# Latent convolution in 32x32 tiles, a layer norm by channels, and sums over blocks by additions

## The chip, the core and the metric

The kernel runs on one core of a Trainium2 chip. A core has engines that work side by side, each with an instruction stream of its own: TensorE (PE, matrix products on a 128x128 array, with a queue for loading the stationary operand, PEld), VectorE (DVE), ScalarE (ACT), GpSimd (POOL) and SyncE (SP), from whose queue nearly all of this kernel's DMA transfers are issued. Engines wait for each other by semaphores. Data lie on chip in SBUF (128 partitions) and in eight PSUM banks (128 partitions x 512 columns of fp32, where matmuls write), off chip in HBM.

The metric is the time of one execution in microseconds on the device, median of the runs. Less is better.

## What is computed

One layer of a hybrid backbone: an SSD branch (bidirectional Mamba-2 scan) and a Conformer branch share one input projection and one output projection. 256 context tokens and 2048 latent tokens go through it, model width D = 1024, so 18 tiles of 128 tokens. Cut to what the change bears on:

```python
u = (rms_norm(x, g_pre) * (1 + scale) + shift) @ w_in
z, xbc, dt_raw, ga, gb, gsil = split(u)            # 1024 channels each but xbc, dt_raw
y_ssd, h_fin = ssd_branch(z, xbc, dt_raw, ...)     # ends in silu(z) * y, rms_norm over channels

def conformer_branch(ga, gb, conv_w, conv_b, ln_g, ln_b):
    h = ga * sigmoid(gb)
    h = depthwise_conv(h, conv_w, conv_b)          # 31 taps, each channel by itself
    h = layer_norm(h, ln_g, ln_b)                  # over the 1024 channels of a token
    return silu(h)

y_conf = conformer_branch(...) * silu(gsil)
out = concat([y_ssd, y_conf]) @ w_out              # 2048 x 1024
return x + gate * rms_norm(out, g_post), h_fin
```

The 31 taps run along the rows of the grid. The latent grid has 32 rows of 64 columns; so for one channel the convolution is a 32x32 band matrix (Toeplitz: the entry depends on the distance of two rows) times a block of 32 rows by 64 columns. The context grid is 256 rows of one column.

## The kernel before

**Projections.** Tokens come in two halves, each a sequence of blocks of up to 512 tokens. A unit takes the 128 weight columns of one group of channels and goes through the blocks: `mm_cm` (L373) issues, for each of the eight pieces of 128 input channels, three matmuls (L378, L379, L380), since weights and activations are split in a high and a low part of type FP32R. The result is channel-major (channels on partitions). `gab_unit` (L528) projects gate and value of 128 channels j of the Conformer branch, multiplies them and stores the product to the DRAM tensor GL[j]; `silu_unit` does z and gsil, stored to ZS and GS. The weights are fetched on SP's queue by `load_w` (L340), up to three units ahead.

**Beside the projections.** The generators of the scan (`pass_a`, L648) and of the convolutions are woven in between projection steps with `merge` and `interleave` (L836 to L866): after so many steps of projection one step of the side work is issued. For the second half (L926 to L942) these are the scan of tiles 9 to 17 and, from the 49th step on, a chain of `lat_conv(0)`, `ctx_conv(4)`, `lat_conv(1)`, `lat_conv(2)` and so on: all eight groups of latent channels and the last four of the context. In the profile this is the stage from about 935 to 1345 us.

**Context convolution,** `ctx_conv` (L580): 31 fused multiply-adds on DVE, channel-major; two transposes on PE (L595); ACT multiplies by 0.5 (L597); a store to CVC, which is token-major (a token's 1024 channels in a row).

**Latent convolution,** `lat_conv(j)` (L603), 128 channels. kd receives the Toeplitz matrices, by reading the padded taps with overlap (L611); x receives the products from GL[j], the 32 rows of one of four channels on each group of 32 partitions (L616). `expand` (L618) has ACT copy the 32x32 matrices of four channels at a time onto the diagonal of a 128x128 tile in kbuf, whose other entries are zero from the start (16 copies per 128 channels, L622). A matmul (L634) then has x of four channels as the stationary operand (128 partitions by 64 grid columns) and a block-diagonal tile as the moving one (128 columns: four channels by 32 rows). Its result takes 64 columns of the array, so two of them, for the two halves h, write to the two halves of a PSUM bank. There are four groups of eight such matmuls per 128 channels. DVE adds the bias and turns the order of the columns (L639). Two stores put vt to CVL (L644), token-major.

**Output phase.** After the projections comes a loop over the token tiles (L1141 to L1168), latent tiles from the last to the first, then the two of the context. In a turn, PE does 96 matmuls of the output projection for tile i (`out_part`, L1073; 16 pieces of 128 channels, three products, two halves of 512 columns) while other engines prepare the next tiles. The text of the loop sets where the work for the next tile stands between them:

- `ssd_pre` (L968) for the tile after the next: inter-chunk term, y times z, Square on ACT (L989), a sum over eight blocks of channels as one reduction on DVE (L991);
- `ssd_norm` (L1001) and `ssd_scale` (L1010): sum over partitions as a matmul with ones into a column (L1004), the power -0.5 on GpSimd (`rstd_of`, L135), its spread over the partitions by a matmul with the identity (L1012), the multiplication (L1013), the split in high and low parts (`ssd_hl`, L1016);
- `conf_pre` (L1037): load of the tile, token-major (n, tag cn, one buffer), mean and variance by `bn_stats` and `bn_aggr` on DVE (L1042, L1044), L135 on GpSimd, and the normalisation with the two columns of each token as scalars (L1047);
- `conf_act` (L1050): eight transposes back to channel-major (L1058), eight activations with Silu, whose scale and bias are the layer norm's weights by channel (L1061), the product with gsil (L1063); v has one buffer;
- `conf_hl` (L1066): split of v, copy on ACT and L1070 on DVE; `finish` (L1081): the output norm and the store.

Before the loop, the first tile's preparation stands between the last projection units (L1119 to L1132).

**What sets the order.** Each engine runs its own instructions in order. The order is not simply that of the text: the kernel is built in a context with `schedule_with_timeline_sim=True`, in which a list scheduler places instructions by their order in the text and by a simulated time at which their inputs are ready. Buffers come free when their last reader is done; a tile of a pool with `bufs=1` can be loaded again only then. PSUM has three banks with the tag "mm" for projections and five with the tag "ss" for everything else.

## Time and profile before

| | |
|---|---|
| runs | 1882.09, 1887.08 and 1880.9 us; median 1882.09 us |
| profiled execution | 1882.2 us, of which the span from first to last instruction is 1880.5 us |
| mean granted TensorE clock | 0.986 |
| busy | PE 1825.6 us (97%), PEld 1504.6, DVE 1188.2 (63%), ACT 839.5 (45%), POOL 269.0 (14%) |
| DMA | 375.29 MB, 200 GB/s in the mean |

How to read it: an engine's busy time is the sum over its instructions, register and branch instructions left out. The span is the profiled execution's, so a sum of costs taken from the trace is to be set against 1882.2 us. L622 is line 622 of the kernel before; a tile is called by its name in the program without its number (kbuf, cx, cn). A row of a group has: line, engine, operation, output and inputs, shapes, count | busy us, mean ns of one | idle time of the engine just before, and what ended it. A row of the timeline has: start and duration in us, engine, line, operation, output and inputs, shapes, count. The duration of a matmul is its latency; matmuls are pipelined and overlap. An fp32 matmul is recorded as two passes, so its counts are twice those of the code; the matmuls of type FP32R and the transposes are one pass each.

### The profile page before, as it was taken

What the parts mean: (1) busy time and instruction counts of PE and PEld (TensorE: products, weight loads), DVE (VectorE), ACT (ScalarE), POOL (GpSimd) and SP (SyncE); (2) the same over time, 40 slices, a digit from 0 to 9 for tenths busy, and PEclk for the clock granted to TensorE, in tenths of its full rate; (3) what the DMA queues carried; (4) which work ended last, traced back from release to release, by engine and by line L of the source; (5) the groups of instructions that cost most, each with busy time, mean ns of one, the idle gap of its engine ahead of it and who ended that gap; (6) DMA issues with size and microseconds to landing.
All of it is one profiled execution on the core that took longest, in us unless ns stands there. A gap on an engine that the chain in (4) does not pass through costs nothing.

```text
span 1880.5 us, 26833 instructions
## 1 busy us (share of the span) xinstructions
PE 1825.6 (97%) x9739; PEld 1504.6 (80%) x9739; DVE 1188.2 (63%) x1699; ACT 839.5 (45%) x1786; POOL 269.0 (14%) x351
## 2 busy tenths in 40 slices
PE   7899999999999999999999899999999999999998
PEld 4788887787887888888877677777887888888887
DVE  2477887776545553577585768655427676766662
ACT  3646424443455441644355666675414232232321
POOL 0002001111111100100001011110013333333220
PEclk9899999999999999999999999999999999999999
DMA  8556575564677754545587897978887655555532
GB/s 302 212 200 198 211 239 179 176 222 155 211 269 225 225 200 169 165 154 188 179 195 215 210 242 194 278 185 234 239 268 239 191 174 173 165 172 173 175 102 78
DMA packets 290400, 375.29 MB, mean 200 GB/s; under 512 B 85206, under 2 KB 187478, under 8 KB 290268
## 3 DMA queue, kind: packets, MB, share of 16 engines
q1 hardware_dynamic: 290268, 373.58, 64.2%
q8 instruction: 77, 1.26, 0.3%
q14 instruction: 55, 0.45, 0.1%
HBM read 243.92 MB, written 129.59 MB: 199 GB/s over the span
## 4 chain that ended last, share of the span: by engine, by line
PE 62%; DMA 5%; ACT 3%; issue 3%; DVE 2%; SPq 2%; POOL 0%; POOLq 0%; DVEq 0%; ACTq 0%
PE op L1078 20%; PE sp L378 6%; PE sp L379 6%; PE sp L380 6%; DMA lb<-lt 3%; PE xp L379 2%; PE xp L378 2%; PE xp L380 2%; PE py L720 2%; PE ga L378 2%; PE ga L380 1%; PE po L727 1%; PE ga L379 1%; PE qo L985 1%; PE gb L378 1%
## 5 line engine op out<-in xcount | busy, mean ns | idle before, releaser
L684 ACT ACTIVATE lb<-lb,WB 128x128 f32<-128x128 f32 x576 | 184.1, 391 | 150.9 <-POOL lb L676 149.0
L378 PE MATMUL sp<-hh,wh 128*128 128x512 f32 (+1 forms) x640 | 239.7, 375 | 2.6 <-DVE sth L550 2.6
L379 PE MATMUL sp<-hl,wh 128*128 128x512 f32 (+1 forms) x640 | 237.0, 370 | 0.0
L380 PE MATMUL sp<-hh,wl 128*128 128x512 f32 (+1 forms) x640 | 236.7, 370 | 0.2 <-DMA wl<-wld 0.2
L676 POOL TENSOR_SCALAR_AFFINE_SELECT lb<-lb 128x512 f32<-128x512 f32 x144 | 108.7, 760 | 749.7 <-ACT el L673 416.1
L378 PE MATMUL xp<-hh,wh 128*128 128x512 f32 (+1 forms) x480 | 179.1, 375 | 6.1 <-ACT wh L353 4.0
L379 PE MATMUL xp<-hl,wh 128*128 128x512 f32 (+1 forms) x480 | 179.1, 373 | 0.2 <-DVE hl L299 0.2
L380 PE MATMUL xp<-hh,wl 128*128 128x512 f32 (+1 forms) x480 | 179.2, 374 | 0.0
L475 DVE SCALAR_TENSOR_TENSOR cva<-raw,cwh,cva 128x1280 f32<-128x1280 f32 (+1 forms) x96 | 142.7, 1495 | 15.5 <-ACT cva L469 13.6
L378 PEld LDWEIGHTS sp<-hh,wh 128*128 128x128 f32 x640 | 121.0, 189 | 24.3 <-DVE sth L550 3.1
L380 PEld LDWEIGHTS sp<-hh,wl 128*128 128x128 f32 x640 | 121.0, 189 | 21.6 <-DMA wl<-wld 0.7
L379 PEld LDWEIGHTS sp<-hl,wh 128*128 128x128 f32 x640 | 121.2, 189 | 20.1 <-issue 0.5
L378 PE MATMUL gb<-hh,wh 128*128 128x512 f32 (+1 forms) x320 | 121.9, 381 | 3.4 <-DVE gth L539 3.4
L378 PE MATMUL ga<-hh,wh 128*128 128x512 f32 (+1 forms) x320 | 120.4, 376 | 2.6 <-ACT gth L536 2.6
L379 PE MATMUL gb<-hl,wh 128*128 128x512 f32 (+1 forms) x320 | 119.3, 373 | 0.0
L380 PE MATMUL gb<-hh,wl 128*128 128x512 f32 (+1 forms) x320 | 119.1, 372 | 0.0
L380 PE MATMUL ga<-hh,wl 128*128 128x512 f32 (+1 forms) x320 | 118.1, 369 | 0.0
L379 PE MATMUL ga<-hl,wh 128*128 128x512 f32 (+1 forms) x320 | 117.9, 369 | 0.0
L590 DVE SCALAR_TENSOR_TENSOR cg<-cg,cv 128x256 f32<-128x256 f32 x240 | 113.3, 497 | 2.5
L550 DVE SCALAR_TENSOR_TENSOR sth<-sth,sp 128x512 f32<-128x512 f32 (+1 forms) x80 | 50.4, 630 | 98.4 <-ACT sth L549 98.4
L378 PEld LDWEIGHTS xp<-hh,wh 128*128 128x128 f32 x480 | 92.0, 192 | 23.0 <-ACT wh L353 4.8
L688 DVE TENSOR_TENSOR lb<-lb,lb 128x512 f32<-128x512 f32 x72 | 51.6, 717 | 85.6 <-ACT lb L684 55.8
(219 smaller groups left out, 3860.8 us busy)
## 6 DMA issues: line engine op xcount, KB each, us to landing
lb<-lt SPq DMA_DIRECT2D x144, 256.0 KB, 4.2
wr<-in_w_in SPq DMA_DIRECT2D x88, 256.0 KB, 4.9
whd<-wh SPq DMA_DIRECT2D x44, 512.0 KB, 3.4
wld<-wl SPq DMA_DIRECT2D x44, 512.0 KB, 4.7
wh<-whd SPq DMA_DIRECT2D x44, 512.0 KB, 5.2
wl<-wld SPq DMA_DIRECT2D x44, 512.0 KB, 5.6
xT<-xb SPq DMA_DIRECT2D x18, 512.0 KB, 5.4
yp<-yg SPq DMA_DIRECT2D x36, 256.0 KB, 4.5
```

Source lines behind the costliest of these rows:

```text
L378: T.matmul(ps[:, :BN], wh[:, k, :], hh[:, k, :], start=(k == 0), stop=False)
L379: T.matmul(ps[:, :BN], wh[:, k, :], hl[:, k, :], start=False, stop=False)
L380: T.matmul(ps[:, :BN], wl[:, k, :], hh[:, k, :], start=False, stop=(k == KT - 1))
L475: V.scalar_tensor_tensor(a[:, :n], raw[:, t:t + n], cwh[:, ct * 5 + t:ct * 5 + t + 1], a[:, :n], MUL, ADD)
L550: V.scalar_tensor_tensor(th, th, 1.0, ps[:, :BN], ADD, MUL)
L590: V.scalar_tensor_tensor(acc, g[:, t:t + 256], cv[:, w0 + t:w0 + t + 1], acc, MUL, ADD)
L676: G.affine_select(E[g, hq, d], E[g, hq, d], pattern=[[0, 4], [sg, P]], compare_op=ALU.is_ge, fill=NEG, base=0, channel_multiplier=-sg)
L684: S.activation(lb[:, h, :], lb[:, h, :], AF.Exp, bias=WB[:, i, c + h:c + h + 1])
L688: V.tensor_tensor(a, a, E[g, hq, 1], ADD)
L720: T.matmul(py[g][j * HD:(j + 1) * HD, q * P:(q + 1) * P], xt[g][:, h * HD:(h + 1) * HD], E[g, hq, 0][:, t, :], start=True, stop=True)
L727: T.matmul(po[g][:, q * P:(q + 1) * P], Sf[g][:, q * P:(q + 1) * P], bc[:, 2 + g, :], start=True, stop=True)
L1078: T.matmul(pso[n], lhs[:, k % 8, :], w[:, n * 512:(n + 1) * 512], start=(k == 0 and m == 0), stop=(k == 15 and m == 2))
```

## The change

1. **Layout.** The results of both convolutions go to one channel-major tensor CV, 1024 channels by 18 x 128 tokens, in place of the token-major CVC and CVL. `ctx_conv` loses its transposes: ACT reads the DVE result in place of a PSUM bank.
2. **Latent convolution.** Each channel has a 32x32 tile of the array. The channels of a block of 128 are dealt out so that channel u*32 + a*8 + q lies on the row group a (partitions 32a to 32a+31) and comes out on the column group u; `wconv` is laid out on the host to fit. The Toeplitz matrix of a channel is the stationary operand (32x32), its 64 grid columns the moving one. Per 128 channels there are two groups (h) of 64 matmuls; in a group, two row groups a and four column groups u alternate from one matmul to the next, and each row group writes to a PSUM bank of its own. One ACT copy per 128 channels reverses the row index (kt), in place of 16 copies to block-diagonal tiles, which go, with the zero fill of kbuf. DVE's evacuations (four per 128 channels) write vt with the columns in their order. x is loaded in 16 pieces per 128 channels (eight channels each), kd in four; the stores are eight. The bias cbb is loaded once for all channels.
3. **Loads ahead.** kd and cx have two buffers. `lat_conv(j)` loads for j + 1 right after its copy, where `gl_done` says that the projection unit of j + 1 was already issued; where not, the next call loads for itself.
4. **Sums over blocks.** `sum8` adds eight blocks of 128 columns in three DVE additions (512, 256 and 128 columns). It stands for the reduction L991, and is used twice in the new layer norm.
5. **Layer norm by channels.** `conf_load` loads the tile channel-major (n). `conf_mean`: sum8, a matmul with a 128x128 matrix of ones, which leaves every token's sum on every partition, and one DVE pass that subtracts the mean over all channels. `conf_var`: Square on ACT into v, sum8, a matmul whose result is a column (tokens on partitions), the power on GpSimd. `conf_scale`: a matmul with the identity spreads it over the partitions again, and a DVE pass multiplies. `conf_act` then needs no transposes: its eight activations read n from SBUF. The statistics by `bn_stats` and L1047 go.
6. **Places in the loop.** For the next tile, `conf_load` stands where `conf_pre` stood; `ssd_scale` comes after five of 16 pieces, not six; `conf_mean` after seven; `conf_var` where `conf_act` stood (after ten); `conf_scale` and `conf_act` after twelve.

Of the 18 tiles, 17 go through the loop's preparation and the first through the one before it.

```diff
--- before.py
+++ after.py
@@ -85,8 +85,7 @@
     ZS = [dram(f"zs{h}", [D, HT[h] * P]) for h in range(2)]
...
     GS = [dram(f"gs{h}", [D, HT[h] * P]) for h in range(2)]
-    CVC = dram("cvc", [NCTX * P, D])
-    CVL = dram("cvl", [LAT, D])
+    CV = dram("cv", [D, NT * P])
     YP = [dram(f"yp{i}", [P, D]) for i in range(NT)]
...
     LT = [dram(f"lt{h}", [HT[h] * 32, P]) for h in range(2)]
@@ -525,9 +524,12 @@
         for _ in dtp:
...
+    gl_done = set()
     def gab_unit(half, j, hb):
...
         wa = next_w()
+        gl_done.discard(j)
         for b in ORDER[half]:
...
             pg = bank("mm", f"gb{half}_{j}_{b}")
@@ -538,6 +540,8 @@
             yield from mm_cm(pa_, wa, hb[b])
...
             DMA.dma_start(GL[j][:, o:o + BN], th)
+        if half:
+            gl_done.add(j)
...
         w = next_w()
@@ -590,59 +594,57 @@
             V.scalar_tensor_tensor(acc, g[:, t:t + 256], cv[:, w0 + t:w0 + t + 1], acc, MUL, ADD)
...
                 yield
-        ps = bank("ss", f"cps{j}")
-        for t in range(2):
-            T.transpose(ps[:, t * P:(t + 1) * P], acc[:, t * P:(t + 1) * P], ident)
         o = g[:, 768:1024]
-        S.mul(o, ps[:, :256], 0.5)
...
+        S.mul(o, acc, 0.5)
+        DMA.dma_start(CV[j * P:(j + 1) * P, 0:256], o)
+        yield
+    lat_in = {}
+    def lat_load(j, lp):
+        kd = lp.tile([P, 32, 32], F32, tag="kd", name=f"kd{j}", bufs=2)
+        x = lp.tile([P, 32, 64], F32, tag="cx", name=f"cx{j}", bufs=2)
+        lat_in[j] = kd, x
+        for a in range(4):
+            rs = slice(a * 32, (a + 1) * 32)
+            src = bass.AP(tensor=wconv.tensor, offset=(j * 4 + a) * 64 * 32, ap=[[32, 32], [1, 1024]])
+            DMA.dma_start(kd[rs].rearrange("p r g -> p (r g)"), src)
+            for u in range(4):
+                c0 = u * 32 + a * 8
+                DMA.dma_start(x[rs, u * 8:(u + 1) * 8, :],
+                              GL[j][c0:c0 + 8, 256:].rearrange("c (r w) -> r c w", w=64))
+    def lat_conv(j, lp, cbb, more):
+        if j not in lat_in:
+            lat_load(j, lp)
+        kd, x = lat_in.pop(j)
+        yield
+        kt = lp.tile([P, 32, 32], F32, tag="kt", name=f"kt{j}", bufs=1)
+        S.copy(kt[:, :, ::-1].rearrange("p g r -> p r g"), kd)
+        if more(j + 1):
+            lat_load(j + 1, lp)
+        yield
+        vt = lp.tile([P, 32, 64], F32, tag="cvv", name=f"cvv{j}", bufs=1)
         for h in range(2):
-            c0 = j * P + h * 64
...
+            ps = {a: bank("ss", f"cp{j}_{a}") for a in (2 * h, 2 * h + 1)}
+            for q in range(8):
+                for u in range(4):
+                    for a in ps:
+                        rs = slice(a * 32, (a + 1) * 32)
+                        T.matmul(ps[a][u * 32:(u + 1) * 32, q * 64:(q + 1) * 64], kt[rs, u * 8 + q, :], x[rs, u * 8 + q, :],
+                                 start=True, stop=True)
             yield
-            V.scalar_tensor_tensor(vt[:, ::-1, u * 16:(u + 1) * 16].rearrange("p r c -> p c r"),
...
+            for a in ps:
+                V.scalar_tensor_tensor(vt[:, a * 8:(a + 1) * 8, :], ps[a].rearrange("p (c w) -> p c w", w=64), 0.5,
+                                       cbb[:, j, a * 8:(a + 1) * 8].unsqueeze(2).to_broadcast([P, 8, 64]), MUL, ADD)
+            for u in range(4):
+                c0 = j * P + u * 32 + h * 16
+                DMA.dma_start(CV[c0:c0 + 16, 256:].rearrange("c (r w) -> r c w", w=64),
+                              vt[u * 32:(u + 1) * 32, h * 16:(h + 1) * 16, :])
+            yield
...
     def pass_a(i):
@@ -926,12 +928,14 @@
     ph_b[0].close()
...
     lp = ph_l.enter_context(tc.tile_pool(name="lp", bufs=1, side="right"))
-    kbuf = [lp.tile([P, 8, P], F32, name=f"kbuf{u}") for u in range(2)]
-    for u in range(2):
-        G.memset(kbuf[u], 0.0)
+    cbb = lp.tile([P, 8, 32], F32, name="cbb")
+    for u in range(4):
+        DMA.dma_start(cbb[u * 32:(u + 1) * 32],
+                      conf_b.rearrange("(j u n) -> u j n", u=4, n=32)[u].partition_broadcast(32))
     blocks = post(1, 5)
     cg = lambda name: lp.tile([P, D], F32, tag="cg", name=name, bufs=2)
-    extra = chain(f for j in range(4) for f in (lat_conv(2 * j, lp, kbuf), ctx_conv(j + 4, cg), lat_conv(2 * j + 1, lp, kbuf)))
+    lat = lambda j: lat_conv(j, lp, cbb, gl_done.__contains__)
+    extra = chain(f for j in range(4) for f in (lat(2 * j), ctx_conv(j + 4, cg), lat(2 * j + 1)))
     sc_ = scan(range(9, NT))
...
     interleave(take(blocks, 24), [sc_] * 4, 24)
@@ -964,6 +968,13 @@
...
     Sb = [p0.tile([P, 512], F32, name=f"Sb{g}") for g in range(2)]
+    def sum8(t, v):
+        V.tensor_tensor(t, v[:, 0:4, :], v[:, 4:8, :], ADD)
+        V.tensor_tensor(t[:, 0:2, :], t[:, 0:2, :], t[:, 2:4, :], ADD)
+        V.tensor_tensor(t[:, 0, :], t[:, 0, :], t[:, 1, :], ADD)
+        return t[:, 0, :]
...
         ct = p1.tile([P, 2, P], F32, tag="ct", name=f"ct{i}", bufs=1)
@@ -987,8 +998,7 @@
             V.tensor_tensor(y, y, el, ADD)
...
         S.activation(z, y, AF.Square)
-        zr = p1.tile([P, P], F32, tag="zr", name=f"zr{i}", bufs=2)
-        V.tensor_reduce(zr, z.rearrange("p q l -> p l q"), mybir.AxisListType.X, ADD)
+        zr = sum8(z[:, 0:4, :], z)
         for g in range(2):
...
             if first:
@@ -1034,32 +1044,44 @@
         DMA.dma_start(t, GGD[a].partition_broadcast(P))
...
-    def conf_pre(i):
...
+    rows8 = lambda t: t.unsqueeze(1).to_broadcast([P, 8, P])
+    def conf_load(i):
+        n = p2.tile([P, 8, P], F32, tag="cn", name=f"cn{i}", bufs=1)
+        DMA.dma_start(n, CV[:, i * P:(i + 1) * P].rearrange("(c p) t -> p c t", p=P))
         return n
-    def conf_act(i, n):
+    def conf_mean(i, n):
+        v = p2.tile([P, 8, P], F32, tag="v", name=f"v{i}", bufs=1)
+        t = sum8(v[:, 0:4, :], n)
+        mean = bank("ss", f"cm{i}")[:, 0:P]
+        T.matmul(mean, ones, t, start=True, stop=True)
+        V.scalar_tensor_tensor(n, rows8(mean), -1.0 / D, n, MUL, ADD)
+        return n, v
+    def conf_var(i, nv):
+        n, v = nv
+        S.activation(v, n, AF.Square)
+        t = sum8(v[:, 0:4, :], v)
+        pq = bank("ss", f"cq{i}")
+        T.matmul(pq[:, 0:1], t, ones[:, 0:1], start=True, stop=True)
+        ms = p2.tile([P, 1], F32, tag="cms", name=f"cms{i}", bufs=2)
+        V.tensor_scalar(ms, pq[:, 0:1], 1.0 / D, EPS, MUL, ADD)
+        return n, v, rstd_of(p2, ms, f"cr{i}"), pq
+    def conf_scale(i, nvr):
+        n, v, r, pq = nvr
+        T.matmul(pq[:, P:2 * P], r.to_broadcast([P, P]), ident, start=True, stop=True)
+        V.tensor_tensor(n, n, rows8(pq[:, P:2 * P]), MUL)
+        return n, v
+    def conf_act(i, nv):
+        n, v = nv
         gs = p2.tile([P, 8, P], F32, tag="gs", name=f"gsl{i}", bufs=1)
         DMA.dma_start(gs, chan_slice(GS, i))
-        v = p2.tile([P, 8, P], F32, tag="v", name=f"v{i}", bufs=1)
...
+        for k in range(8):
+            S.activation(v[:, k, :], n[:, k, :], AF.Silu, bias=cv[:, C_LNB + k:C_LNB + k + 1],
+                         scale=cv[:, C_LNG + k:C_LNG + k + 1])
         V.scalar_tensor_tensor(v, v, 0.5, gs, MUL, MUL)
...
@@ -1124,12 +1146,12 @@
             if b == 1 and n == 0:
...
                 p2 = ph_1.enter_context(tc.tile_pool(name="p2", bufs=1))
-                gap(p2, 192)
+                gap(p2, 64)
                 yh = ssd_scale(i, yr)
-                nrm = conf_pre(i)
+                nrm = conf_mean(i, conf_load(i))
     for u in last:
         run(u)
-    v = conf_act(i, nrm)
+    v = conf_act(i, conf_scale(i, conf_var(i, nrm)))
     ph_b[2].close()
...
     p3 = ph_1.enter_context(tc.tile_pool(name="p3", bufs=1))
@@ -1150,18 +1172,23 @@
         if a + 2 < NT:
...
         if not last:
-            n = conf_pre(nxt)
-        out_part(pso[i], yh, 3, 6)
+            n = conf_load(nxt)
+        out_part(pso[i], yh, 3, 5)
         if not last:
             yhn = ssd_scale(nxt, yr)
-        out_part(pso[i], yh, 6, 8)
+        out_part(pso[i], yh, 5, 7)
+        if not last:
+            n = conf_mean(nxt, n)
+        out_part(pso[i], yh, 7, 8)
         out_part(pso[i], pt, 8, 10)
...
         else:
-            v = conf_act(nxt, n)
-            out_part(pso[i], pt, 10, 16)
+            n = conf_var(nxt, n)
+            out_part(pso[i], pt, 10, 12)
+            v = conf_act(nxt, conf_scale(nxt, n))
+            out_part(pso[i], pt, 12, 16)
             yh = yhn
...
             load_gg(1)
@@ -1199,7 +1226,7 @@
     )
...
     wpad[:, 16:16 + CW] = a["conf_conv_w"][0].T
-    wconv = wpad.reshape(8, 32, 4, 64).transpose(0, 2, 3, 1)
+    wconv = wpad.reshape(8, 4, 4, 8, 64).transpose(0, 2, 4, 1, 3)
     xa = np.concatenate([a["x_prompt"][0], a["x_sample"][0]], axis=0)
...
     arrays = {
```

57 lines of the change are left out of this document (removed).

## The prediction

> **What bounds the kernel now.** First the page: busy times, and the chain that ended last by engine.
>
> ```profile
> PE 1825.6 (97%) x9739; PEld 1504.6 (80%) x9739; DVE 1188.2 (63%) x1699; ACT 839.5 (45%) x1786; POOL 269.0 (14%) x351
> ...
> PE 62%; DMA 5%; ACT 3%; issue 3%; DVE 2%; SPq 2%; POOL 0%; POOLq 0%; DVEq 0%; ACTq 0%
> ```
>
> TensorE (PE) sets the end; no other engine is near. So a change is worth the PE time that it frees, plus the PE waits that it ends, less those that it makes. Next the windows view, for the stages that the change touches: columns are length, busy us (instructions) of PE, PEld, DVE, ACT, POOL, granted clock, DMA share, GB/s.
>
> ```profile
> 935.00:1345.00 410.00, 392.55 (x2333) 308.38 (x2333) 272.90 (x448) 251.96 (x564) 42.55 (x64) 0.98 0.82 220
> 1425.00:1455.00 30.00, 26.40 (x117) 21.13 (x116) 28.43 (x27) 14.48 (x22) 11.37 (x8) 0.89 0.85 250
> 1460.00:1860.00 400.00, 400.00 (x1962) 336.47 (x1961) 263.61 (x310) 114.63 (x239) 119.13 (x103) 1.00 0.52 161
> ```
>
> In the stage with the latent convolution (935 to 1345) PE stands still for 410.0 - 392.6 = 17.4 us, and its mean clock of 0.98 costs 0.02 x 410 = 8 us more. In the output loop (1460 to 1860) PE never waits. Between them (1425 to 1455) VectorE (DVE) is busy 28.4 of 30 us and PE waits 3.6. Third, the groups of instructions.
>
> ```profile
> L622 ACT COPY kbuf<-kd 32x256 f32<-32x256 f32 x128 | 83.3, 657 | 19.6 <-DMA kd<-in_wconv 11.8 <-PE cp L634 6.0
> ...
> L634 PE MATMUL cp<-kbuf,cx 128*64 128x128 f32 x512 | 37.1, 291 | 12.4 <-ACT kbuf L622 10.0 <-DMA cx<-gl 1.9 <-DVE cvv L639 0.3
> ...
> L991 DVE TENSOR_REDUCE zr<-z 128x128 f32<-128x1024 f32 x18 | 36.2, 2011 | 1.1 <-ACT z L989 1.1
> ...
> L1013 DVE TENSOR_TENSOR y<-y,pm 128x1024 f32<-128x1024 f32 x18 | 21.8, 1209 | 2.9 <-PE pm L1012 2.9
> ...
> L1047 DVE TENSOR_SCALAR cn<-cn,mv,cr 128x1024 f32<-128x1024 f32 x18 | 14.6, 813 | 11.1 <-POOL cr L135 11.1
> ```
>
> 256 convolution matmuls are 512 passes (each FP32 matmul runs as two). PE idled 12.4 us right before them, 10.0 of it for ScalarE (ACT), which spreads the weights into block-diagonal tiles: 128 copies, 83.3 us.
>
> **Term 1, the convolution on PE.** A pass's duration here is a latency; the price is read from starts, around one group of 16 passes.
>
> ```profile
> 957.30 0.39 PE L379 MATMUL ga<-hl,wh 128*128 128x512 f32 x1
> 957.53 0.39 PE L380 MATMUL ga<-hh,wl 128*128 128x512 f32 x1
> 957.85 1.09 PE L634 MATMUL cp<-kbuf,cx 128*64 128x128 f32 x16
> 958.87 0.50 PE L378 MATMUL ga<-hh,wh 128*128 128x512 f32 x1
> 959.21 0.40 PE L379 MATMUL ga<-hl,wh 128*128 128x512 f32 x1
> ```
>
> Projection matmuls start 0.23 us apart (the first two rows), two of them 0.45. Without the group, two such steps would lie between 957.53 and 959.21: 1.68 - 0.45 = 1.23 us. There are 32 groups: 39.4 us.
>
> Afterwards there are 16 groups of 64 matmuls, 128 passes each, with 64 moving columns in 32x32 tiles; eight tiles (two row groups by four column strips) lie next to each other in the order. No row shows row groups. The nearest show column strips; the windows view again, PE and PEld only. First matmuls of 128 columns on the whole array, one at a time:
>
> ```profile
> 1508.70:1510.40 1.70, 1.69 (x16) 1.69 (x15) 1.00 0.00 0
> ```
>
> Then matmuls of 256 columns in four strips, at the start of the kernel (L239):
>
> ```profile
> 23.80:25.31 1.51, 1.51 (x32) 0.67 (x28) 1.00 1.01 370
> ```
>
> One at a time, 128 columns take 1.70/16 = 0.106 us. Four strips start 28 to 32 passes of 256 columns in 1.51 us, about 0.05 each, where alone one would take 0.21: strips run fully side by side. Half as many columns are 0.053 us; eight at once make 128 x 0.053 / 8 = 0.85 us per group, only four at once 1.70. I take 1.15, nearer to full overlap, as the four-strip row loses nothing. Entering and leaving the tiled mode cost 1.23 - 8 x 0.106 = 0.38 now; I keep it. 16 x 1.53 = 24.5 us, so **-15 us** (bounds -20 and -6).
>
> The Trainium skill (TensorE: Matmul & The Clock Gate, Part 3) measured 10.6 times the speed of one tile for sixteen tiles. By that share, an estimate, 0.85 would be 1.28 us per group, and the term 2 us smaller; no run here shows it.
>
> **Term 2, the waits for the weights.** The 128 copies become eight, one per 128 channels, each 1024 columns (not over four of the old copies of 256, 2.6 us), and issued a step ahead, and the next inputs load a block early where they exist. Of the 10.0 us I take 9 as gone, and 5 of the 8 us of clock, taking it that its dips follow stops (from 1425 to 1455 PE waits 3.6 us, and the clock is 0.89): **-14 us** (bounds 0, if another wait stands behind, and -18). What is late next is the scan between the same matmuls, whose masks wait for DMA; the DMA share is 0.82. ACT falls from 252 to about 190 of 410 us (83 less, eight times 2.6 more), and the evacuations lose their stride; neither engine is the bound, so that alone gives nothing.
>
> The loads are cut finer: per 128 channels 28 issues on SP stand for 12. The row of the queue for the inputs (min/median/max ns):
>
> ```profile
> L616 SPq DMA_DIRECT2D cx<-gl x32: 325/637/2844, 946.1 to 1290.8; - x32
> ```
>
> Bytes and pieces (256 B) stay. At the smallest, 0.325, sixteen input loads take 5.2 us where 4 x 0.64 = 2.5 stand, and eight stores for two at most 2.6 more: up to 5 us per block, 42 in 410. I cost it at nothing, hidden behind weights that are fetched three deep; without that cover, 42 is the bound.
>
> **Term 3, the context convolution** loses two transposes eight times. Two passes put among the projections cost 0.23 (worked out below): **-1.8 us**.
>
> **Term 4, PE in the output loop.** Per token tile eight transposes go; a sum over partitions, a column for the variance and a spread of the scale come, two passes each.
>
> ```profile
> 1505.29 0.62 PE L1078 MATMUL op<-woh,yl 128*128 128x512 f32 x2
> 1505.74 0.28 PE L1004 MATMUL pm<-ones,zr 128*128 128x1 f32 x2
> 1505.88 0.71 PE L1078 MATMUL op<-woh,yh 128*128 128x512 f32 x2
> 1506.43 0.39 PE L1078 MATMUL op<-wol,yh 128*128 128x512 f32 x1
> ...
> 1519.84 0.62 PE L1078 MATMUL op<-woh,pl 128*128 128x512 f32 x2
> 1520.30 1.03 PE L1058 MATMUL ct<-ident,cn 128*128 128x128 f32 x8
> 1521.09 0.70 PE L1078 MATMUL op<-woh,ph 128*128 128x512 f32 x2
> 1521.63 0.40 PE L1078 MATMUL op<-wol,ph 128*128 128x512 f32 x1
> ```
>
> Four long matmuls are 0.91 us. Two short passes cost 1506.43 - 1505.29 - 0.91 = 0.23, the transposes 1521.63 - 1519.84 - 0.91 = 0.88. So 3 x 0.23 - 0.88 = -0.19, times 17 tiles: **-3.3 us**.
>
> **Term 5, the chain of the norm.** Two answers of the timeline, of PE and of the loop, show first that the order is a planner's, not the text's:
>
> ```profile
> 984.06 0.48 PE L378 MATMUL ga<-hh,wh 128*128 128x512 f32 x1
> 984.94 0.30 PE L696 MATMUL px<-ident,xT 128*128 128x128 f32 x1 [0.40 <-issue]
> ```
>
> L696 cuts into a triple of projection matmuls that is written without a break.
>
> ```profile
> 1502.25 1.29 DVE L1042 BATCH_NORM_STATS2 bs<-cn 128x6 f32<-128x512 f32 x2 [2.09 <-DMA cn<-cvl]
> ...
> 1505.36 1.22 DVE L1070 TENSOR_TENSOR pl<-v,ph 128x1024 fp32r<-128x1024 f32 x1
> ```
>
> L1042 of the next tile runs before L1070, though it is written after it.
>
> DVE now does 1.29 us of statistics and the pass of L1047, 0.81: 2.1 us, and some on single columns, before and after, which I leave out. Then come two sums over blocks and two passes of 1.21 (L1013). A sum is three additions of 512, 256 and 128 columns: 1.06 us by columns from L1013, 1.94 if each cost as much as one L1042 of 512 columns (0.65); I take 1.4, as those two show that an instruction grows with its columns. Per tile 2 x 1.4 + 2 x 1.21 - 2.1 = +3.1, and a sum in place of the 2.01 of L991 takes 0.6 back: +2.5, so DVE goes from 16.5 to 19.0 of 25 us. ACT has one square more, about a pass; with 115 of 400 us it hides that. The loads come in pieces of 512 B, not 4 KB, under a DMA share of 0.52: nothing.
>
> PE stays the bound on average; but three matmuls now wait for a chain through DVE, ACT and GpSimd, where there was one block of transposes whose input was ready long before. A matmul whose input is late in the plan is put later, between long ones, and the wait shrinks to the plan's error: I take 0.35 us per tile, **+6 us** (bounds 0 and the 4.6 per tile of the rival below).
>
> **Term 6, the turn to the output loop**, where DVE is full: 2.5 us more for one tile, **+2 us** (bounds 0 and +5).
>
> Sum: -15 - 14 - 1.8 - 3.3 + 6 + 2 = -26 us. The profiled execution took 1882.2 us (1880.5 of span, 1.7 around it), like the median of 1882.1; **forecast 1856 us**, by itself 1842 to 1870.
>
> **Rivals.**
> *The waits stay.* The scan's waits take the place of the copies', and term 2 is nothing: 1856 + 14 = 1870. For it, a DMA share of 0.82 over the whole stage; against it, 10.0 us with ACT's copy named.
> *Small passes don't come faster.* The two L1004 passes of a tile, with one column each, stand within 0.28 us (above); the durations of all of them (min/median/max ns) are:
>
> ```profile
> L1004 PE MATMUL pm<-ones,zr x36: 164/208/250, 1397.4 to 1828.9; 128*128 128x1 f32 x36
> ```
>
> So the second starts at most about 0.28 - 0.25 = 0.03 us after the first if it is the long one. At 0.027 each, 128 passes are 3.4 us: 16 x 3.8 = 61, 36 more than in term 1: 1892. Against it, the four-strip row: 0.05 for 256 columns is no floor yet. It decides from 128 x + 0.38 = 3.1, about 0.02 us a pass. The Trainium skill (TensorE: Matmul & The Clock Gate, Part 1) has such a floor, about 25 ns from start to start however few the columns; by that rule this rival is the result, and the trace agrees for one tile.
> *PE waits for the norm: slower.*
>
> ```profile
> 1507.80:1520.00 12.20, 12.20 (x64) 10.43 (x63) 12.05 (x10) 2.11 (x2) 6.96 (x4) 1.00 0.63 183
> ```
>
> The first sum needs v free, and v is read until L1070 ends (1506.6), and the next input, whose single buffer comes free only after the activations. If it misses the gap before 1510, the SSD steps, written earlier, keep DVE until 1520.0 (12.05 of 12.20 us busy), less 0.6, and the sum is done at 1520.8. In the text its matmul stands three parts (six long matmuls, 1.36 us each) before where the transposes are: 1520.3 - 4.1 = 1516.2. That is 4.6 us per tile, 78 in 17 tiles: 1856 - 6 + 78 = 1928. It decides from 32/17 = 1.9 us per tile. For it, DVE is full there; against it, the planner's order.
>
> **Chances.** Forecast 0.52, waits stay 0.18, small passes 0.09, norm 0.21 (a third of it near 2 us a tile, about no change). About 0.3% is what a measurement of this kernel can tell. Faster by over 0.3%: the first two less their tails, 0.68; within: 0.12; slower: 0.20. The range runs from term 1 and 2 at their best (1840) to just past the small-pass rival, 1893; the norm at full price is left out.
>
> **What would show it.** Term 1: a group of 128 passes from start to start in 1.2 to 1.9 us. Term 2: no idle time before the convolution for its weights, clock near 1.00 from 1000 to 1200. Term 4 and 5: 24.8 to 25.2 us from tile to tile in the loop; 27 or more, with PE waiting for a sum, would prove the third rival, and a group of over 3 us the second.

## The result and the profile after

The changed kernel takes 2006.6 us in the median (1998.7 to 2011.6); the ratio to the kernel before is 1.0651, 95% interval 1.0607 to 1.0696. Its profiled execution took 2002.9 us, 2001.1 of it span, 120.6 more than before. First the page: busy times, and the chain that ended last by engine.

```profile
PE 1858.5 (93%) x11223; PEld 1518.2 (76%) x11223; DVE 1201.7 (60%) x1807; ACT 795.8 (40%) x1684; POOL 257.4 (13%) x349
...
PE 75%; DVE 8%; DMA 6%; issue 4%; ACT 3%; SPq 2%; POOL 2%; POOLq 0%; DVEq 0%; ACTq 0%
```

PE fell from 97% to 93% of a longer span, and no other engine's share rose: nobody is the bound by its amount of work, so engines wait for each other. The windows of the changed kernel (length, busy us and instructions of PE, PEld, DVE, ACT, POOL, granted clock, DMA share, GB/s), the convolution stage and a stretch of the output loop, show where:

```profile
935.00:1345.00 410.00, 375.89 (x3802) 297.42 (x3801) 254.64 (x442) 178.00 (x438) 44.20 (x64) 0.95 0.77 214
1580.00:1980.00 400.00, 346.25 (x1530) 278.91 (x1528) 222.05 (x320) 107.55 (x207) 79.71 (x78) 0.91 0.46 125
```

In the loop PE was busy all of 400.0 us; now it stands still for 53.8 of them, and the granted clock is 0.91 instead of 1.00. In the convolution stage it stands still for 34.1 us instead of 17.4, at 0.95 instead of 0.98. To weigh the stages, the timelines of PE at three places: the same projection matmul ahead of the convolution stage and behind it, and the start of the output matmuls. The kernel before:

```profile
954.36 0.39 PE L378 MATMUL gb<-hh,wh 128*128 128x512 f32 x1
...
1352.47 0.39 PE L380 MATMUL sp<-hh,wl 128*128 128x512 f32 x1
...
1422.27 0.71 PE L1078 MATMUL op<-woh,yh 128*128 128x512 f32 x2
```

The kernel after, the same matmuls by their number in the order of the projections (its line numbers differ: L377 to L379 are L378 to L380 of before, L1100 is L1078):

```profile
946.15 0.39 PE L377 MATMUL gb<-hh,wh 128*128 128x512 f32 x1
...
1357.19 0.39 PE L379 MATMUL sp<-hh,wl 128*128 128x512 f32 x1
...
1424.15 0.39 PE L1100 MATMUL op<-woh,yh 128*128 128x512 f32 x1
```

Before the stage the changed kernel is 8.2 us ahead, behind it 4.7 us late: the stage itself, with cheaper matmuls in it, lost 12.9 us. The output matmuls begin 1.9 us late, and from there to the end of the span are 577.0 us against 458.2: **118.7 us are lost in the output phase**. One turn of the loop takes 31.4 us instead of 25.0 (14 turns between the evacuations of L1116 at 1502.7 and 1942.6). What PE waited for in that phase (us in total, times, longest):

```profile
PE op L1100 <- ACT yh L1029: 56.7, 17, 6.3
PE op L1100 <- ACT ph L1091: 17.8, 10, 4.4
PE op L1100 <- DVE yl L1030: 3.7, 8, 1.1
```

PE doesn't wait for the norm's own matmuls. It waits, once in every turn, for the next tile's high part of y (yh), which comes from the SSD branch and not from the norm. The timelines of one turn show why. The lines of the changed kernel: L1051 load of n, L974 the first addition of a sum, L1058 matmul of the mean, L1059 its subtraction, L1064 square, L1067 matmul of the variance, L1075 product with the spread scale, L1083 activations, L1092 and L1091 split of v, L1023 the SSD norm's product that completes y, L1029 cast of y to yh. On DVE (start, length, what ran, idle time before it and what ended that):

```profile
1671.23 1.22 DVE L1092 TENSOR_TENSOR pl<-v,ph 128x1024 fp32r<-128x1024 f32 x1
...
1673.04 0.69 DVE L974 TENSOR_TENSOR v<-cn 128x512 f32<-128x512 f32 x1 [0.26 <-DMA cn<-cv]
...
1678.87 1.23 DVE L1059 SCALAR_TENSOR_TENSOR cn<-cm,cn 128x1024 f32<-128x1024 f32 x1 [4.27 <-PE cm L1058]
1681.28 0.69 DVE L974 TENSOR_TENSOR v<-v 128x512 f32<-128x512 f32 x1 [1.19 <-ACT v L1064]
...
1682.46 0.29 DVE L976 TENSOR_TENSOR v<-v 128x128 f32<-128x128 f32 x1
1687.64 0.16 DVE L1069 TENSOR_SCALAR cms<-cq 128x1 f32<-128x1 f32 x1 [4.88 <-PE cq L1067]
...
1692.51 1.22 DVE L1075 TENSOR_TENSOR cn<-cn,cq 128x1024 f32<-128x1024 f32 x1
...
1695.50 1.21 DVE L1023 TENSOR_TENSOR y<-y,pm 128x1024 f32<-128x1024 f32 x1
...
1701.80 1.21 DVE L1092 TENSOR_TENSOR pl<-v,ph 128x1024 fp32r<-128x1024 f32 x1
1702.93 0.68 DVE L974 TENSOR_TENSOR z<-z 128x512 f32<-128x512 f32 x1
1704.60 0.69 DVE L974 TENSOR_TENSOR v<-cn 128x512 f32<-128x512 f32 x1 [0.99 <-DMA cn<-cv]
```

On PE, the start after the stop, and the norm's two sums:

```profile
1669.31 0.80 PE L1100 MATMUL op<-woh,yh 128*128 128x512 f32 x1 [4.73 <-ACT yh L1029]
...
1678.44 0.38 PE L1058 MATMUL cm<-v,ones 128*128 128x128 f32 x2
...
1687.33 0.28 PE L1067 MATMUL cq<-ones,v 128*128 128x1 f32 x2
```

On ACT, in the same turn:

```profile
1693.82 3.19 ACT L1083 ACTIVATE v<-cn,cv 128x128 f32<-128x128 f32 x8 [4.29 <-DVE cn L1075]
1696.91 1.03 ACT L1029 CAST yh<-y 128x1024 fp32r<-128x1024 f32 x1
```

And the loads of n on SP's queue:

```profile
1668.35 0.38 SPq L1051 DMA_DIRECT2D cn<-cv  x1
...
1697.83 0.39 SPq L1051 DMA_DIRECT2D cn<-cv  x1
```

This is a ring. The first sum of the next tile (1673.04) needs v, free when L1092 has read it (1672.4), and n, which is loaded only after the activations have read its one buffer (issue at 1668.35). From there come mean, square, sum, variance, spread, product, activations (1693.82), gate, split (1701.80), and at 1704.60 the next sum: 31.6 us in this turn. The work in it is short; DVE stood idle 4.27 us for the matmul of the mean and 4.88 for that of the variance, whose places on PE come late: the sum for the mean was done at 1674.60 and its matmul started at 1678.44, the sum for the variance at 1682.75 and its matmul at 1687.33. And since the activations stand ahead of the cast of yh on ACT (1696.91), the next tile's first products wait with the ring. But that place on ACT is only a third of it. Taken over all 17 waits for yh by the ends of L1023 and the starts of L1029, PE waited 19.1 of the 56.7 us while y itself was not complete, 20.0 while the cast stood behind the activations, and 17.6 during the cast. The turns alternate: in the one shown y was complete at 1696.71, 0.2 us before its cast, in the one before it 2.0.

### The profile page after: what moved, and what is told of

Read it like the earlier page. It is cut to its first block, busy times and chain, and to the rows that moved or that the text cites. A ratio compares the mean times of both kernels' runs of the same rounds, so it can differ in the third digit from the quotient of the medians.

```text
span 2001.1 us, 29974 instructions
## 1 busy us (share of the span) xinstructions
PE 1858.5 (93%) x11223; PEld 1518.2 (76%) x11223; DVE 1201.7 (60%) x1807; ACT 795.8 (40%) x1684; POOL 257.4 (13%) x349
## 4 chain that ended last, share of the span: by engine, by line
PE 75%; DVE 8%; DMA 6%; issue 4%; ACT 3%; SPq 2%; POOL 2%; POOLq 0%; DVEq 0%; ACTq 0%
PE op L1100 15%; PE sp L377 6%; PE sp L378 6%; PE sp L379 6%; PE xp L377 5%; PE xp L379 5%; PE xp L378 5%; PE ga L377 3%; PE ga L379 3%; PE gb L377 3%; PE ga L378 3%; PE gb L379 3%; PE gb L378 3%; DMA lb<-lt 2%; PE py L722 2%
## 5 line engine op out<-in xcount | busy, mean ns | idle before, releaser
L377 PE MATMUL sp<-hh,wh 128*128 128x512 f32 (+1 forms) x640 | 239.6, 374 | 0.0
L378 PE MATMUL sp<-hl,wh 128*128 128x512 f32 (+1 forms) x640 | 237.2, 371 | 0.0
L379 PE MATMUL sp<-hh,wl 128*128 128x512 f32 (+1 forms) x640 | 236.9, 370 | 0.0
L377 PE MATMUL xp<-hh,wh 128*128 128x512 f32 (+1 forms) x480 | 178.4, 373 | 4.1 <-ACT wh L352 2.8
L379 PE MATMUL xp<-hh,wl 128*128 128x512 f32 (+1 forms) x480 | 178.2, 372 | 0.0
L378 PE MATMUL xp<-hl,wh 128*128 128x512 f32 (+1 forms) x480 | 178.2, 372 | 0.0
L1100 PE MATMUL op<-woh,yh 128*128 128x512 f32 x288 | 115.0, 447 | 56.7 <-ACT yh L1029 56.7
L377 PEld LDWEIGHTS sp<-hh,wh 128*128 128x128 f32 x640 | 121.4, 190 | 20.8 <-DVE sth L554 0.2
L379 PEld LDWEIGHTS sp<-hh,wl 128*128 128x128 f32 x640 | 121.3, 190 | 20.9
L378 PEld LDWEIGHTS sp<-hl,wh 128*128 128x128 f32 x640 | 121.6, 190 | 20.0
L377 PE MATMUL gb<-hh,wh 128*128 128x512 f32 (+1 forms) x320 | 122.3, 382 | 4.1 <-DVE gth L541 4.1
L377 PE MATMUL ga<-hh,wh 128*128 128x512 f32 (+1 forms) x320 | 121.5, 380 | 0.1
L378 PE MATMUL gb<-hl,wh 128*128 128x512 f32 (+1 forms) x320 | 120.4, 376 | 0.0
L379 PE MATMUL gb<-hh,wl 128*128 128x512 f32 (+1 forms) x320 | 120.2, 376 | 0.0
L379 PE MATMUL ga<-hh,wl 128*128 128x512 f32 (+1 forms) x320 | 118.7, 371 | 0.5 <-DMA wl<-wld 0.5
L378 PE MATMUL ga<-hl,wh 128*128 128x512 f32 (+1 forms) x320 | 118.8, 371 | 0.0
L1100 PEld LDWEIGHTS op<-woh,yh 128*128 128x128 f32 x288 | 60.3, 212 | 74.6 <-ACT yh L1029 63.5
L1100 PE MATMUL op<-woh,yl 128*128 128x512 f32 x288 | 112.2, 434 | 3.8 <-DVE yl L1030 3.7
```

Source lines behind the costliest of these rows:

```text
L377: T.matmul(ps[:, :BN], wh[:, k, :], hh[:, k, :], start=(k == 0), stop=False)
L378: T.matmul(ps[:, :BN], wh[:, k, :], hl[:, k, :], start=False, stop=False)
L379: T.matmul(ps[:, :BN], wl[:, k, :], hh[:, k, :], start=False, stop=(k == KT - 1))
L1100: T.matmul(pso[n], lhs[:, k % 8, :], w[:, n * 512:(n + 1) * 512], start=(k == 0 and m == 0), stop=(k == 15 and m == 2))
```

## The experiments

The expectations were on record ahead of each run. Ratios are to runs of the kernel before on the same chip; its median on the chips used lies between 1877.8 and 1882.4 us, so a few us between two runs of different chips mean little.

**Which half loses the time.** conv_only has the new convolutions and the old norm and loop, norm_only the reverse. In both, the norm reads the same bytes in the shapes of its half, but the rows aren't tokens or channels, so the output is not the reference's.

```diff
 conv_only, conf_pre of the old norm:
-        DMA.dma_start(n, CVC[i * P:(i + 1) * P, :] if i < 2 else CVL[(i - 2) * P:(i - 1) * P, :])
+        DMA.dma_start(n, CV.rearrange("c t -> (c t)").rearrange("(r d) -> r d", d=D)[i * P:(i + 1) * P, :])
 norm_only, conf_load of the new norm, CV being CVC and CVL in one tensor:
+        cm_ = CV.rearrange("t c -> (t c)").rearrange("(c t) -> c t", t=NT * P)
+        DMA.dma_start(n, cm_[:, i * P:(i + 1) * P].rearrange("(c p) t -> p c t", p=P))
```

> New convolutions and channel-major store, old layer norm, old reduction, old loop; the norm reads the same bytes in the same shapes as before but out of the channel-major tensor, so its rows aren't tokens. Theory (the layer norm alone costs the time, and the convolution part gains nothing, because what it frees on PE is lost to waits for PSUM banks and DVE in that stage): output loop back at 25.0 us per tile, the projections end as late as in the changed kernel (about 1424 us), so 1882 to 1890 us. Rival (the convolution part gains what was forecast, and the changed loop disturbs even the stage before): 1850 to 1862 us.

> Old convolutions, new layer norm by channels, sums by additions and new loop; the norm reads the token-major tensor in channel-major shapes, so its rows aren't channels. Theory (the loop alone loses): loop at 31 us per tile, about 1995 us (1985 to 2010). Rival (the loop loses only together with the new convolution's stores): under 1930 us.

conv_only: 1884.8 us, ratio 1.0025 (1.0013 to 1.0037). norm_only: 2000.3 us, 1.0637 (1.0610 to 1.0665). The norm, with its places in the loop, loses nearly all of it; the convolution gains nothing.

**Which buffers close the ring.** One, the other, or both doubled:

```diff
-        n = p2.tile([P, 8, P], F32, tag="cn", name=f"cn{i}", bufs=1)
+        n = p2.tile([P, 8, P], F32, tag="cn", name=f"cn{i}", bufs=2)
...
-        v = p2.tile([P, 8, P], F32, tag="v", name=f"v{i}", bufs=1)
+        v = p2.tile([P, 8, P], F32, tag="v", name=f"v{i}", bufs=2)
```

> The changed kernel with two buffers for n. Theory (the loop turns in a ring that is closed twice, by the one buffer of n and by the one buffer of v; freeing one leaves the other): still about 31 us per tile, 1995 to 2010 us. Rival (the load of n, 4.7 us from issue to landing, after the activations of the tile before is the loss): 17 x 4.7 = 80 us less, about 1927 us.

> The changed kernel with two buffers for v and one for n. Theory (either buffer closes the ring): about 31 us per tile, 1990 to 2010 us. Rival (v alone closes it): under 1940 us.

> The changed kernel with two buffers for n and for v. Theory (the ring over both buffers sets 31 us per tile): the ring is open, PE is the bound again but for waits between the last steps of the norm and the next tile's products; 26 to 27.5 us per tile, 1915 to 1945 us. Rival (ScalarE's order, eight activations ahead of the cast of yh, or VectorE's burst of work at the turn's start, whichever buffers there are): 30 us per tile or more, 1985 us or more.

n2: 2000.8 us, 1.0641 (1.0624 to 1.0658). v2: 1997.0, one run. nv2: 1917.2, 1.0187 (1.0167 to 1.0207), with 26.4 us per turn in the mean (turns of 22.5 and 30.3 alternate from 1500 to 1786). Either buffer alone leaves the ring closed, both open it. A second buffer also lets the planner move the steps, so these runs show that the single buffers are needed for the loss, and not how the 6.4 us divide among the steps of the ring. With both, PE's waits from 1500 to 1800 are small and for another thing, the last steps of the norm:

```profile
PE op L1100 <- DVE pl L1092: 6.7, 6, 1.1
PE op L1100 <- ACT ph L1091: 5.8, 12, 0.6
```

**Is it the places?** p3 keeps both buffers and begins the norm a tile ahead, so that each of its matmuls has its input long before; the p3_coarse below adds coarser transfers.

```diff
+    nm = conf_mean(order[1], conf_load(order[1]))
     for a, i in enumerate(order):
...
+        out_part(pso[i], yh, 3, 4)
+        if not last:
+            nm = conf_var(nxt, nm)
...
+        out_part(pso[i], pt, 8, 9)
+        if not last:
+            v = conf_act(nxt, conf_scale(nxt, nm))
...
+        if a + 2 < NT:
+            nm = conf_mean(order[a + 2], nl)
```

> The changed kernel with two buffers for n and v, and the norm begun a tile ahead: load, sum and mean for the tile after the next late in a turn, variance after 4 and scale and activations after 9 of 16 pieces of the following one. Theory (the ring over buffers and places is all of the loop's loss; nothing in the norm's work itself needs more than 25 us of an engine): 24.8 to 25.2 us per tile, no wait of PE in the loop, 1885 to 1895 us. Rival (VectorE's and ScalarE's order still makes PE wait 1 us or more per tile): 1905 us or more.

p3: 1887.9 us, 1.0053 (1.0029 to 1.0077); a turn takes 24.87 us (ten turns between the evacuations at 1522.7 and 1771.4), less than the 25.0 of before. The window of p3 in the loop:

```profile
1460.00:1800.00 340.00, 338.09 (x1649) 283.86 (x1648) 278.08 (x369) 119.48 (x225) 131.74 (x97) 0.99 0.61 178
```

DVE has 278 us in 340, 20.3 per turn, and PE stands still for 1.9: the norm by channels needs no more than there is. Its ring was too long, not its work.

**Why the convolution stage gains nothing.** The matmuls cost about what was forecast. PE's timeline of the changed kernel around one group:

```profile
957.42 0.40 PE L379 MATMUL ga<-hh,wl 128*128 128x512 f32 x1
957.75 1.49 PE L637 MATMUL cp<-cx,kt 32*32 32x64 f32 x128
959.17 0.50 PE L377 MATMUL ga<-hh,wh 128*128 128x512 f32 x1
959.51 0.40 PE L378 MATMUL ga<-hl,wh 128*128 128x512 f32 x1
```

From 957.42 to 959.51 are 2.09 us where two steps, 0.45, would be without the group: 1.64, reckoned as in the prediction. Twelve of the 16 groups are like this; the other four stop inside until VectorE or ScalarE has emptied a PSUM bank. So PE has less to do and waits more. Measured between the two projection matmuls shown above, ahead of the stage and behind it, the stage takes 398.1 us before and 410.5 to 414.7 in the six kernels with the changed kernel's convolutions (after, conv_only, n2, v2, nv2 and p3). What DVE waited for in this stage (us in total, times, longest), one line of the changed kernel, where the kernel before had 17.9 us:

```profile
DVE yg L758 <- DMA yp<-yg: 28.2, 9, 7.9
```

The scan has two buffers for yg and writes one again only when its store has landed. Those stores stand in SP's queue among the 16 loads of x and eight stores per 128 channels. conv_coarse deals the channels to the tiles in another order, so that four loads and four stores do; conv_l16 and conv_s8 cut these again.

```diff
 conv_coarse:
-            for u in range(4):
-                c0 = u * 32 + a * 8
-                DMA.dma_start(x[rs, u * 8:(u + 1) * 8, :],
-                              GL[j][c0:c0 + 8, 256:].rearrange("c (r w) -> r c w", w=64))
+            DMA.dma_start(x[rs], GL[j][:, 256:].rearrange("(g c) (r w) -> c r g w", c=4, w=64)[a])
...
-                V.scalar_tensor_tensor(vt[:, a * 8:(a + 1) * 8, :], ps[a].rearrange("p (c w) -> p c w", w=64), 0.5,
+                V.scalar_tensor_tensor(vt[:, a::4, :], ps[a].rearrange("p (c w) -> p c w", w=64), 0.5,
 conv_l16, on top of it, in place of the one load:
+            xs = GL[j][:, 256:].rearrange("(g c) (r w) -> c r g w", c=4, w=64)[a]
+            for u in range(4):
+                DMA.dma_start(x[rs, u * 8:(u + 1) * 8, :], xs[:, u * 8:(u + 1) * 8, :])
```

> As conv_only (new convolutions, old layer norm and loop; the norm's rows aren't tokens), but the channels are dealt to the tiles in another order, so that x comes in 4 transfers per 128 channels instead of 16 and goes out in 4 instead of 8; bytes and matmuls are the same. Theory (the finer transfers hold up SyncE's queue: the scan's stores of yg wait behind them, VectorE waits for those stores, PE for VectorE): the scan's stores come earlier, and 8 to 20 us of the stage are won back, 1862 to 1877 us. Rival (the stage waits for PSUM banks, two of which a group of 64 matmuls holds, or for a worse order of VectorE): no gain, 1880 to 1890 us.

> As conv_coarse (1868 us), with each of its four loads of x cut in four: 16 loads and 4 stores per 128 channels, the same bytes, rows and matmuls. Theory A (the number of loads costs the stage its gain): 1878 to 1890 us, as conv_only. Theory B (the loads don't matter, the stores or the order do): 1864 to 1873 us.

> As conv_coarse, with each of its four stores cut in two: 4 loads and 8 stores per 128 channels. Theory A (the loads count): 1864 to 1873 us. Theory C (the stores count): 1878 to 1890 us.

conv_coarse: 1868.4 us, 0.9946 (0.9930 to 0.9963). conv_l16: 1889.9, 1.0043 (1.0027 to 1.0059). conv_s8: 1871.1, 0.9958 (0.9941 to 0.9975). With 16 loads of x in place of four the kernel takes about 20 us more, with eight stores in place of four no more than the two medians vary. The difference lies in the stage, 394.9 us in conv_coarse, 396.4 in conv_s8 and 417.1 in conv_l16. That the loads do it by themselves isn't shown, because the planner's order moves with them: counted from the traces, 35 of VectorE's 1699 instructions stand in another order in conv_l16 than in conv_coarse, 15 in conv_s8. DVE's wait for the stores of yg, in conv_l16:

```profile
DVE yg L757 <- DMA yp<-yg: 30.1, 7, 11.6
```

And in conv_coarse:

```profile
DVE yg L755 <- DMA yp<-yg: 18.2, 6, 5.6
```

One of them in conv_l16, on SP's queue:

```profile
1239.36 3.96 SPq L645 DMA_DIRECT2D cv<-cvv  x4
1243.36 7.06 SPq L617 DMA_DIRECT2D cx<-gl  x7
1250.52 0.40 SPq L555 DMA_DIRECT2D zs<-sth  x1
1250.96 2.94 SPq L617 DMA_DIRECT2D cx<-gl  x6
1254.00 0.39 SPq L751 DMA_DIRECT2D st<-sb  x1
1254.44 0.43 SPq L765 DMA_DIRECT2D yp<-yg  x1
```

And on DVE:

```profile
1241.55 0.69 DVE L764 TENSOR_TENSOR yg<-yg,yo 128x512 f32<-128x512 f32 x1
...
1257.67 0.69 DVE L757 TENSOR_TENSOR yg<-xT,dcol 128x512 f32<-128x512 f32 x1 [8.73 <-DMA yp<-yg]
```

yg was done at 1242.2, its store left at 1254.44 behind the 13 loads and the stores that are shown, and DVE, whose next step needs that buffer, stood still for 8.7 us with the scan's other work behind it.

**Is that store the whole path?** l16_gyp moves the stores of yg to GpSimd's queue in conv_l16, p3_gyp does so in p3_coarse, and conv_tiny adds to conv_coarse twelve loads of 128 bytes per 128 channels.

```diff
 l16_gyp, p3_gyp:
-            DMA.dma_start(YP[i][:, g * 512:(g + 1) * 512], y.rearrange("p q l -> p (q l)"))
+            G.dma_start(YP[i][:, g * 512:(g + 1) * 512], y.rearrange("p q l -> p (q l)"))
 conv_tiny, behind each load of x:
+            for u in range(3):
+                DMA.dma_start(dm[0][a * 32:a * 32 + 1, j % 2, u], wconv[j, a, u:u + 1, :])
```

> conv_l16 (16 loads of x per 128 channels, 1890 us) with one line changed: the scan's stores of yg are issued from GpSimd's queue instead of SyncE's. Theory (16 loads hurt because those stores stand behind them in SyncE's queue): the stores leave within 3 us, VectorE's wait for them goes from 34 to under 15 us, and the time to 1868 to 1876 us, as with 4 loads. Rival (the pieces crowd the DMA engines, or the masks and weights that queue on SyncE are as late): 1884 us or more.

> p3_coarse (1872 us) with the stores of yg on GpSimd's queue. Theory: what is left of VectorE's wait for them (17 us) goes for the most part: 1858 to 1868 us, over 0.5% faster than the kernel before. Rival (GpSimd, which then waits for VectorE before each store, makes its masks late, and the scan with them): 1872 us or more.

> conv_coarse (1868 us) with three more loads of 128 bytes behind each load of x, into a tile that nothing reads: 16 issues per 128 channels for loads around x, as in conv_l16 (1890 us), but next to no bytes and no later x. Theory (SyncE's time for issuing, about 0.35 us each and 34 us in all, delays what is queued behind): 1880 to 1892 us. Rival (it is the transfers themselves, their pieces or their late landing, not the queue): 1865 to 1873 us.

l16_gyp: 1899.6 us, 1.0116 (1.0098 to 1.0135), slower still. DVE's wait for the store fell as expected, from 30.1 to 7.3 us with 13.6 put down to "issue", but GpSimd now stood before those stores itself, with the scan's masks queued behind them (its waits in the stage):

```profile
POOL yp L765 <- DVE yg L764: 55.8, 9, 22.8
```

p3_gyp: 1877.5, 0.9996 (0.9978 to 1.0013), no gain either. Since both give GpSimd a wait of its own, they don't tell what the stage would do with early stores alone. conv_tiny: 1880.5, 1.0006 (0.9989 to 1.0022): with issues of next to no bytes added, the kernel lost some 11 of the 20 us, and DVE's wait for the stores of yg was only 15.2 us there. So those stores are not the whole path. The run points to the issues on SP's queue as a cost, but here too the order moved (70 of VectorE's 1699 instructions against conv_coarse), and that rival is not ruled out; what else carries the loss, and the remaining 9 us, stay open. p3_k1 speaks against a price per issue:

> p3_coarse (1872 us, ratio 0.996) with kd in one load per 128 channels instead of four: 24 issues less. Theory (issues on SyncE cost, about 20 us for 96): 2 to 6 us less, ratio 0.993 to 0.995. Rival: as p3_coarse within 2 us.

It took 1892.4 us, 1.0082 (1.0054 to 1.0110), 20 us more than p3_coarse with 24 issues less, and with only 14 of VectorE's 1807 instructions in another order. Its first convolution waited 9.1 us for x, whose loads began to leave at 949.26, where they do so at 942.60 in p3_coarse: behind the load of kd, SP's queue stood still for 6.8 us, put down to the landing of a store to GL. No run isolates a cause for the other half of the 20 us. So a loss of this size also comes with four loads of x, and neither the number of issues nor the number of instructions that moved foretells it. No run holds the order fixed.

**What holds two row groups apart, and what the stage costs in all.**

```diff
 conv_bank1 (with the store after the last of four):
-        for h in range(2):
-            ps = {a: bank("ss", f"cp{j}_{a}") for a in (2 * h, 2 * h + 1)}
+        for h in range(4):
+            ps = {h: bank("ss", f"cp{j}_{h}")}
 no_lat:
-    extra = chain(f for j in range(4) for f in (lat(2 * j), ctx_conv(j + 4, cg), lat(2 * j + 1)))
+    extra = chain(f for j in range(4) for f in (iter(range(6)), ctx_conv(j + 4, cg), iter(range(6))))
```

> As conv_coarse, with one row group of the array at a time: 32 groups of 32 matmuls, each into one PSUM bank, instead of 16 groups of 64 into two. If only the four column strips run side by side then, and the work limits: 64 passes take as long as 128 did (1.26 us), a group 1.49, in all 47.7 us instead of 23.8, so 1892 us. If passes start one after the other at about 10 ns whatever lies beside: 0.64 per group, 27.8 us in all, so 1872 us. If holding two banks made the scan wait, up to 8 us less than either.

> conv_coarse without the latent convolution: no loads, copies, matmuls, evacuations or stores of it; six empty steps stand in its places, and the norm reads another written tensor in the same shape. It shows what the scan waits for by itself. If the waits in the stage are the scan's own: only the 24 us of matmuls go, 1842 to 1848 us. If they are the convolution's doing: another 15 to 20 us, 1824 to 1830 us.

conv_bank1: 1877.5 us, 0.9991 (0.9978 to 1.0003), 9 more than conv_coarse and between the two prices. One of its groups on PE's timeline:

```profile
956.41 0.40 PE L379 MATMUL ga<-hh,wl 128*128 128x512 f32 x1
956.74 1.09 PE L634 MATMUL cp<-cx,kt 32*32 32x64 f32 x64
957.76 0.50 PE L377 MATMUL ga<-hh,wh 128*128 128x512 f32 x1
958.10 0.40 PE L378 MATMUL ga<-hl,wh 128*128 128x512 f32 x1
```

1.69 us less 0.45 are 1.24 for 64 passes, 40 us for all 32 groups against 26 for 16 of 1.64. By PE's time alone that is 13 us more; 9 were measured. No price of holding two banks can be read from the 4 us between, since 100 of VectorE's 1699 instructions stand in another order and the last seven groups follow each other without projections between them. no_lat: 1817.7, 0.9670 (0.9651 to 0.9689), 51 us under conv_coarse, where the matmuls are 26, and under both forecasts. PE never stands still in its stage. So about 25 us of waits and slower clock hang on the latent convolution even with coarse transfers; that the waits are the scan's own (1842 to 1848) is out.

**A version that beats both kernels,** the kernel before by 0.4%: p3 with the transfers of conv_coarse.

> p3 and the coarser transfers of conv_coarse together. Theory: both gains, 1862 to 1880 us, faster than the kernel before. Rival (no gain from the transfers): as p3.

p3_coarse: 1872.1 us, 0.9962 (0.9949 to 0.9976). In its loop PE never stands still:

```profile
1460.00:1800.00 340.00, 340.00 (x1666) 285.82 (x1664) 272.86 (x362) 118.54 (x224) 123.46 (x93) 1.00 0.58 173
```

## Why the prediction was wrong

*Term 5, the chain of the norm, failed.* It took 0.35 us per tile, "the wait shrinks to the plan's error"; the turn grew by 6.4 us. The planner did put the matmuls behind their inputs (3.8 and 4.6 us behind them in the turn shown), and PE doesn't wait at them. But in a loop that doesn't dissolve a wait: every step that is put later makes the next tile's first sum later, because n and v have one buffer each, and what is left is the length of the ring, 31 us. n2, v2 and nv2 show the ring, p3 that with buffers and places mended the same work fits into 24.87 us. The amounts were right and beside the point: a sum of three additions takes 0.69 + 0.42 + 0.29 = 1.40 us, as was taken, and DVE's 19.0 us per turn are near the 20.3 of p3.

*The rival "PE waits for the norm" had the place and too small a price.* It named v, read until the split, and the single buffer of n, but let the loop start fresh in every turn: 4.6 us, 1928 in all. It also expected PE to wait at the norm's sum; PE waited at yh, for a third of that time behind the activations on ACT, for another third because y itself came late. With 0.21 it was the likeliest rival, and the range left its full price out. The range's lower end is off, too: terms 1 and 2 at their best are 9 us better than the forecast, 1847 and not 1840; nothing hangs on it.

*Term 1 held in its price,* 1.64 us per undisturbed group; 1.53 was forecast. The rival "small passes don't come faster" is out: 128 passes lie between 957.75 and 959.17, under 0.012 us each. The floor of the Trainium skill (TensorE: Matmul & The Clock Gate, Part 1), about 25 ns from start to start, doesn't hold here for passes that go to different tiles of the array in turn.

*Term 2, -14 us, failed, and with it the nothing that the finer loads were costed at.* ACT's copies are gone as a cause, but idle time grew from 17.4 to 34.1 us and the clock fell. The cover that I named, weights fetched three deep, was the wrong one: behind the loads in SP's queue stood the scan's stores and loads, too. conv_l16 against conv_coarse puts about 20 us on them and on the order that came with them, within the bound of 42. "The waits stay" came nearest for this stage: the scan's waits took the place of the copies', and conv_only stands at 1.0025, 5 us more, where terms 1 to 3 had 31 us less; so the forecast would have failed without the norm, too. Even in conv_coarse the stage is only 3.2 us shorter than before; the rest of that run's gain arises ahead of the stage, which it enters 10.4 us early. Why so little of terms 1 and 2 is kept there stays open.

*Term 3* came out larger: where only the first four context convolutions lie, ahead of the stage, the changed kernel is 8.2 us early (6.0 to 10.7 in the other five kernels with its convolutions), for a forecast of 0.9. 2.9 us of that norm_only has too, which keeps the transposes; how the rest divides between the transposes and a changed order, no run tells. *Term 4*, -0.19 per turn, is met by p3's 24.87 against 25.0. *Term 6* can't be read by itself: the last projections and the loop run into each other.

## What to carry to other kernels

When a chain of steps in a loop grows, first add up the ring of each buffer with one copy, from its fill over every engine and every matmul's place to the next fill, and set that beside the turn; an engine with time to spare doesn't help, and a planner that moves late matmuls back lengthens the ring. Transfers that are cut finer can be paid by whatever stands behind them on the same queue, so list that before they are costed at nothing. And where a planner sets the order, a change of transfers changes the order as well; the cause isn't shown until the order is held fixed. A gain on the bounding engine is kept only if what else it runs in that stage, here the scan, can come earlier too.

## What the hardware showed beside this

Passes of 64 columns in 32x32 tiles take next to nothing each where they alternate between tiles: from the first start of a group to the next projection matmul are 1.42 us for 128 passes on eight tiles (957.75 to 959.17), 0.011 us a pass with entry and exit, and 1.02 us for 64 passes on four (956.74 to 957.76), 0.016. And a stop of PE once a turn costs more than its length: PE's waits in the output phase add up to 80.5 us, where the kernel before has 3.6, so they account for 77 of the 118.7 us lost. The other 42, by subtraction, go with slower matmuls: the granted clock over 400 us of the loop was 0.91, against 1.00 in the same loop without stops, and behind the stop that ends at 1669.31 the output matmuls start 0.43 us apart from 1671.4 to 1673.9, and 0.23 from 1674.3 on.
